# Feed-forward in sevens: one modulation step per pair, two thirds of the steps in the down projection, and the queries' reload in eight parts

## The chip, the cores and the metric

The program runs on one core of one Trainium2 chip. The metric is the time of one execution on the device, in microseconds; the median of three executions is given, and one more execution was recorded by the hardware profiler. Times inside an execution count from its first instruction.

## The reference

Two transformer blocks stand one behind the other on 1024 tokens of width 1024, all in float32. Cut to what the change touches:

```python
# block 1, its feed-forward (D_FF = 2816 = 22 tiles of 128)
xn = rms_norm(x, ffn_norm_g)
gate, up = jnp.split(xn @ w_gate_up, 2, axis=-1)
x = x + (jax.nn.silu(gate) * up) @ w_down
# block 2
mod = silu(c) @ w_mod + b_mod            # 6 vectors of 1024; 2 of them also for c_ctx
h = modulate(rmsnorm(x, norm1_g), sh1, sc1)
q, k, v, u, gb, gc, ga, gcv = split_projection(h @ w_in)
o = latent_window_attention(rope(q), rope(k), v, k_ctx, v_ctx, sink)
y = gb * conv3(gc * u)                   # short convolution
x = x + g1 * ((sigmoid(ga) * (o @ w_proj_attn) + sigmoid(gcv) * (y @ w_proj_conv)) @ w_out)
x = x + g2 * expert_choice_moe(modulate(rmsnorm(x, norm2_g), sh2, sc2), ...)
return rmsnorm(x, final_norm_g)
```

## The kernel before, in words

Everything is written out by hand: the order of the program is the order in which each engine's queue, the DMA queues of SP and GpSimd among them, is worked off. An engine goes on as soon as what its next instruction waits for is there. A matrix product in float32 is three products of parts: every operand is split into a high part (ScalarE, L58) and a rest (VectorE, L59), and `mm3` (L64 to L67) issues high x high, high x rest and rest x high. `Weights` holds the weights' pipeline: SP loads them into stage tiles (L132), `conv` splits them into `wh` and `wl`, `ahead` units before TensorE needs them.

The stages around the change, in order:

- **Gate-up** (L1186 to L1240). The 22 hidden tiles `hr` are made one after the other, f = 0 to 21. The first three (f < `NCL`) are plain products. From f = 3 on a tile and its gate are made as a pair by `quads` (L314): a 2 x 2 block product in seven products of quarters (12 matmuls each, 84 for a pair) instead of eight. Sums of the weights' quarters are GpSimd's (`seven`, L158 to L164), the sums of the seven results VectorE's (L319 to L324 and `plus`, L335), the factor `rsb` GpSimd's again (L1227), the Silu ScalarE's (L1231). The last two products that make the hidden tile (`hidden_out`, L1149 and L1150) are written a pair later (`flush`); then GpSimd stores it to `d_h`. For the last tile they come after the loop.
- **Modulation.** `w_mod` has twelve column blocks s of 512. A step is one load of two row tiles (`mod_load`, L1098, SP's queue, two buffers `mw`) and its use: per row tile one VectorE operation on an accumulator `acc` (L1109 or L1111). For s < 4 there are two accumulators, so a step is four operations, else two. Four steps make a column block; then `mod_sum` lets TensorE add over the partitions (L1120, eight passes for each accumulator) and VectorE add the bias (L1121). `mod_next` uses the step loaded last and loads the next. In the pairs `mods1` does it after product 1, and for f < 11 after product 3 as well, until 24 of the 48 steps are loaded.
- **Down projection** (L1271 to L1302). The hidden tiles come in five parts of 5, 5, 4, 4 and 4. Each part is loaded from `d_h` (`h_load`, three buffers), split (`h_in`) and multiplied with its rows of `w_down`, four columns of 128 at a time (`c0` = 0 and 4, called a chunk below), in pieces of two tiles (`p0` = 0, 2, 4) by `columns_k` (L288). All eight banks are added into `x1` at the end of a chunk (L1288). Between the columns c = 1 and 3 of a piece `mod_next` or, in the second chunk, `step` (split of the next part's tiles) is called; after each chunk follow the sums that are due. The last part is a stage of its own (L1362), for which the modulation must be there.
- **End of the convolution** (L1548 to L1577). In the last four pairs of products (`j` = 0 to 3, gates of the merge) the eight tiles y of the convolution are loaded back from `d_y` (`y_load`, L1553, SP's queue; two buffers, named `z` and `y`) and split (`y_split`).
- **Projection of the convolution** (L1647 to L1674). `gc_load` loads gates on SP's queue. GpSimd's queue loads the keys `kn`, the queries `qn` (4 MB in one transfer, L1651), masks, and later the values `v`. The first two columns are made by `columns_k`, the others by `columns`; `prep_k` and `prep_q` prepare the attention that follows at 1905 us.

Of the kernel before, what the change touches and what calls it, by code (L numbers as in the profile page):

```python
# [8 lines left out]
F32 = mybir.dt.float32  # L9
F32R = mybir.dt.float32r  # L10
# [8 lines left out]
P = 128  # L19
# [3 lines left out]
def fused(tc, x, mix_norm_g, w_in, b_f, sgu_ln_g, sgu_ln_b, w_s, b_s, out_norm_g, w_out,  # L23
# [4 lines left out]
    nc = tc.nc  # L28
# [4 lines left out]
    NT = T // P  # L33
# [1057 lines left out]
        rstd_of(rs1, ss1, D)  # L1091

    modq, modr = deque(), deque()
    acc_of = {}

    def mod_load(s, k):
# [4 lines left out]
    def mod_use(s, k, t):  # L1101
        for j in ((0, 1) if s < 4 else (0,)):
            if k == 0:
                acc_of[s, j] = pmo.tile([P, 512], F32, name=f"acc{j}", bufs=2 - j)
            a = acc_of[s, j]
            for kk in range(2):
                sc = s2[:, k + kk, j:j + 1]
                if k + kk == 0:
                    DVE.tensor_scalar(a, t[:, kk, :], sc, None, op0=OP.mult)  # L1109
                else:  # L1110
                    DVE.scalar_tensor_tensor(a, t[:, kk, :], sc, a, op0=OP.mult, op1=OP.add)  # L1111
        if k == 6:
            modr.append(s)
# [41 lines left out]
    def stores():  # L1155
        while stored:
            stored.popleft()()

    def mod_next(left=0):

        if mwq:
            mod_use(*mwq.popleft())
        if len(modq) > left:
            mod_load(*modq.popleft())

    def early(f):
        if f < FF - 1:
            W.presum()
        else:
            for _ in range(2):  # L1170
                h_load(next(nxt))
# [8 lines left out]
    def mods1():  # L1180

        if modr:
            mod_sum(modr.popleft())
        mod_next(24)

    for f in range(FF):  # L1186
        hr_ = phr.tile([P, T], F32, name="hr")

        def ev_gate(hf, ps):
            g = hr_[:, hf * 512:(hf + 1) * 512]  # L1190
            DVE.tensor_tensor(g, rsb[:, hf * 512:(hf + 1) * 512], ps, op=OP.mult)
            act(g, g, AF.Silu)

        def ev_up(hf, ps):
            g = hr_[:, hf * 512:(hf + 1) * 512]
            DVE.tensor_tensor(g, g, ps, op=OP.mult)
            DVE.tensor_tensor(g, g, rsb[:, hf * 512:(hf + 1) * 512], op=OP.mult)

        if f == 0:
            columns_k(W, 2, xh, xhl, range(KD), lambda c, hf, ps: (ev_gate, ev_up)[c](hf, ps),  # L1200
                      mid={(FM[0], 1): ffn_rs, (FM[1], 1): lambda: spread(rsb, rs1), (FM[2], 1): lambda: W.prime(1)})
            es_fw.close()
            es_x1.close()
            es_T = ExitStack()
            pT = pool(es_T, "pTx", 1, R)
            TX.update({i: quarter(pT, f"t{i}") for i in (4, 1, 2, 3)})
        elif f < NCL:
            columns(W, xh, xhl, KD, ev_gate)
            quarters_x(2 * f - 2)
            if f == NCL - 1:  # L1210
                W.ahead = 4
            columns(W, xh, xhl, KD, ev_up)
            quarters_x(2 * f - 1)
            if f == NCL - 1:
                es_12.close()
                pmo = pool(es_mo, "pmo", 2)
                op = lambda t: [(lambda k, a=a: a[:, k, :]) for a in t]
                SEVX = [op(XQ[0, 0]), op(XQ[1, 0]), op(TX[2]), op(TX[1]), op(TX[3]), op(XQ[1, 1]), op(TX[4])]
        else:
            if f == FF - 1:  # L1220
                W.ahead = 2
            while flush:
                flush.popleft()()
            c1, c2 = halft("c1"), halft("c2")

            def times(x, cs):
                POOL.tensor_tensor(x, x, rsb[:, cs], op=OP.mult)  # L1227
                return x

            def gate(x, cs):  # L1230
                act(x, times(x, cs), AF.Silu)  # L1231

            su = {}
            quads(W, SEVX, halft, lambda s, b: gate(plus(c1, s, b), h0),
                  lambda u, b: (gate(plus(u, u, b), h1), su.update(u=u)),
                  lambda s, b: (times(plus(s, s, b), h0), su.update(s=s)), lambda s, b: times(plus(c2, s, b), h1),
                  {1: mods1, 2: lambda: (stores(), early(f)), **({3: mods1} if f < NCL + 8 else {})})
            flush.append(lambda hr_=hr_, c1=c1, c2=c2, su=su, f=f: hidden_out(hr_, c1, c2, su, f))
        if f < NCL:
            nc.gpsimd.dma_start(d_h[f], hr_)  # L1240
    while flush:
        flush.popleft()()
    W.spare.clear()
    stores()
    assert len(modq) == 24 and not modr and not mwq
    es_mo.close()
    es_xq.close()
    es_T.close()
    es_s1.close()

# [2 lines left out]
    x1 = [px1.tile([P, T], F32, name=f"x1_{k}") for k in range(KD)]  # L1253
    rs1b = px1.tile([P, T], F32, name="rs1b")
    phh = pool(es_f, "phh", 5, R)
    pmo = pool(es_mo, "pmo2", 2)

    def h_split():
        h, l = phh.tile([P, T], F32R, name="hH"), phh.tile([P, T], F32R, name="hL")
# [4 lines left out]
    def h_in():  # L1264
        r = h_split()
        for f in nxt:
            h_load(f)
            break
        return r

    hTs = []  # L1271
    for i, (f0, n) in enumerate(parts):
        hT = [h_in() for _ in range(n)] if not i else hTs
        hv = lambda i: (lambda k, hf: hT[k][i][:, hf * 512:(hf + 1) * 512])
        if f0 + n == FF:
            break
        for c0 in (0, 4):
            if not i:
                for k in range(c0, c0 + 4):
                    nc.gpsimd.dma_start(x1[k], d_xs[k])  # L1280
            hn, nn = [], parts[i + 1][1]

            def step(p0):

                while len(hn) < min(nn, p0 + 5 - n):
                    hn.append(h_in())

            columns_k(W, 4, hv(0), hv(1), range(n), lambda c, hf, ps: DVE.tensor_tensor(  # L1288
                x1[c0 + c][:, hf * 512:(hf + 1) * 512], x1[c0 + c][:, hf * 512:(hf + 1) * 512], ps, op=OP.add), 2,
                mid={(p0, c): (lambda p0=p0: step(p0)) if c0 and c == 3 else mod_next for p0 in range(0, n, 2) for c in (1, 3) if i or c0})  # L1290
            if c0:
                step(n)

            while modr:
                mod_sum(modr.popleft())
        hTs = hn
    while modq or mwq:
        mod_next()
# [251 lines left out]
    def y_load():  # L1550
        k = len(ys) + len(yraw)
        t = pcv.tile([P, T], F32, name="y") if k % 2 else pcv.tile([P, T + 2], F32, name="z")[:, :T]
        nc.sync.dma_start(t, d_y[k])  # L1553
        yraw.append(t)

    def y_split():
# [90 lines left out]
    bank = lambda: psb.tile([P, 512], F32, name="b")  # L1647
    gc_load(0)
    gc_load(1)
    nc.gpsimd.dma_start(kn, d_kv[:, :, :256])  # L1650
    nc.gpsimd.dma_start(qn, d_q)  # L1651
    nc.gpsimd.dma_start(mk, amask_h)
    nc.gpsimd.dma_start(mk0[:, :256], amask_h[:, :256])
    nc.gpsimd.dma_start(mk0[:, 256:], amask_h[:, 384:])
# [9 lines left out]
    columns_k(W, 2, yr, yrl, range(KD), ev_mc)  # L1664
    for j in range(2, 8):
        gc_load(j)
        columns(W, yr, yrl, KD, lambda hf, ps: ev_mc(j, hf, ps))
        for t in ((2 * j - 4, 2 * j - 3) if j < 7 else ()):
            v_in(t)
        if j in (3, 4, 5):  # L1670

            prep_k(0, 4 * j - 12, bank)
        if j == 6:
            prep_q(0, 0, 0, bank)  # L1674
# [625 lines left out]
```

## Time and profile before

| | us |
|---|---|
| median of three executions | 3029.29 (3028.01 to 3029.31) |
| profiled execution | 3026.69 |
| its span, first to last instruction | 3024.9 |
| TensorE busy | 2842.8 (94%) |
| VectorE busy | 2093.8 (69%) |
| ScalarE busy | 1414.8 (47%) |
| GpSimd busy | 851.4 (28%) |
| mean granted TensorE clock | 0.971 of full speed |

In the profile PE is TensorE, DVE is VectorE, ACT is ScalarE, POOL is GpSimd, SP is SyncE; a q behind a name is the engine's queue. Matmuls are pipelined: one starts 0.227 us after the other and is shown 0.39 us long, so that starts are to be compared with starts.

### The profile page before, as it was taken

The numbers are of one execution on the slowest core, as the hardware profiler recorded it, in microseconds if no ns is written. First come the engines' busy times: TensorE is split into PE (matmuls) and PEld (weight loads), VectorE is DVE, ScalarE is ACT, GpSimd is POOL, SyncE is SP. The second block draws the span as 40 slices with busy tenths as digits, with TensorE's granted clock in tenths as the row PEclk, the third lists the DMA queues.
The fourth block names the chain that finished last, engine by engine and source line by source line (L and its number), as shares of the span: only waits on it lengthen the run. The fifth ranks groups of instructions, "written<-read, shape, count | busy, mean of one in ns | idle before, by whom it ended". The sixth has DMA issues, their size and how long they took to land.

```text
span 3024.9 us, 37545 instructions
## 1 busy us (share of the span) xinstructions
PE 2842.8 (94%) x13715; PEld 2366.9 (78%) x13715; DVE 2093.8 (69%) x2925; ACT 1414.8 (47%) x2241; POOL 851.4 (28%) x797
## 2 busy tenths in 40 slices
PE   8999999978999899999999998899999889999996
PEld 7887878767777778778888887777778768888885
DVE  4446844877776456776766652789742479999998
ACT  5346933222222211431333331688721468888886
POOL 1301312355566100325444421133221301211113
PEclk9999999989999999999999999999999899999998
DMA  5120143223332544232222256000254589999997
GB/s 199 36 77 22 41 148 98 81 95 104 105 102 89 202 164 140 91 137 86 91 84 84 84 175 216 21 20 17 83 177 145 194 315 371 377 372 377 377 377 281
DMA packets 303880, 472.76 MB, mean 156 GB/s; under 512 B 15260, under 2 KB 144000, under 8 KB 303568
## 3 DMA queue, kind: packets, MB, share of 16 engines
q1 hardware_dynamic: 281216, 391.27, 37.5%
q0 software_dynamic: 20992, 78.04, 7.4%
q8 instruction: 108, 1.77, 0.2%
q10 hardware_dynamic: 1488, 1.06, 0.1%
q14 instruction: 76, 0.62, 0.1%
HBM read 396.35 MB, written 73.96 MB: 155 GB/s over the span
## 4 chain that ended last, share of the span: by engine, by line
PE 46%; DVE 5%; ACT 2%; DMA 2%; issue 2%; POOL 1%; POOLq 0%; SPq 0%; DVEq 0%; ACTq 0%
PE b L67 13%; PE b L66 13%; PE b L65 13%; PE pt L1760 1%; PE b L2141 1%; PE po L1790 1%; DVE pl L1778 1%; DVE wl L59 1%; DVE sm L1741 1%; PE po L1791 1%; DVE qs L1645 1%; DMA z<-d_y 1%; PE b L1983 0%; DMA ot<-d_o 0%; PE sp L1730 0%
## 5 line engine op out<-in xcount | busy, mean ns | idle before, releaser
L59 DVE TENSOR_TENSOR wl<-wst,wh 128x1024 fp32r<-128x1024 f32 (+2 forms) x677 | 768.9, 1163 | 209.3 <-ACT wh L58 201.4
L58 ACT ACTIVATE wh<-wst 128x1024 fp32r<-128x1024 f32 (+2 forms) x677 | 610.8, 921 | 406.8 <-PE b L66 210.5
L65 PE MATMUL b<-wh,a 128*128 128x512 f32 x768 | 302.0, 393 | 0.2 <-ACT a L58 0.2
L66 PE MATMUL b<-wl,a 128*128 128x512 f32 x768 | 299.4, 390 | 0.8 <-DVE wl L59 0.8
L67 PE MATMUL b<-wh,a 128*128 128x512 f32 x768 | 299.3, 390 | 0.4 <-DVE a L59 0.4
L2183 POOL DMA_INDIRECT d_x<-b,idxT x15 | 65.8, 4387 | 470.7 <-DVE b L2177 470.7
L67 PEld LDWEIGHTS b<-wh,a 128*128 128x128 f32 x768 | 144.2, 188 | 31.0 <-DVE a L59 1.1
L66 PEld LDWEIGHTS b<-wl,a 128*128 128x128 f32 x768 | 144.4, 188 | 30.4 <-DVE wl L59 1.6
L65 PEld LDWEIGHTS b<-wh,a 128*128 128x128 f32 x768 | 144.5, 188 | 29.6 <-ACT a L58 0.7
L65 PE MATMUL b<-xn,wh 128*128 128x512 f32 x368 | 145.0, 394 | 7.3 <-ACT xn L58 6.4
L67 PE MATMUL b<-xn,wl 128*128 128x512 f32 x368 | 144.4, 393 | 2.0 <-DVE wl L59 2.0
L66 PE MATMUL b<-xn,wh 128*128 128x512 f32 x368 | 144.4, 392 | 0.5 <-DVE xn L59 0.5
L65 PE MATMUL b<-hH,wh 128*128 128x512 f32 x352 | 140.5, 399 | 4.4 <-DVE x L1288 2.3
L66 PE MATMUL b<-hL,wh 128*128 128x512 f32 x352 | 139.2, 395 | 4.0 <-DVE hL L59 4.0
L67 PE MATMUL b<-hH,wl 128*128 128x512 f32 x352 | 139.0, 395 | 0.0
L1111 DVE SCALAR_TENSOR_TENSOR acc<-mw,s,acc 128x512 f32<-128x512 f32 x112 | 114.5, 1031 | 23.8 <-DMA mw<-in_w_mod_dram 21.6
L59 DVE TENSOR_TENSOR wl<-ws,wh 128x512 fp32r<-128x512 f32 x78 | 53.5, 688 | 79.8 <-ACT wh L58 79.8
L1741 DVE CUSTOM_DVE_ANT_0 sm<-sp,mk,nsk 128x640 f32<-128x640 f32 (+1 forms) x128 | 107.1, 838 | 1.5 <-PE sp L1730 1.3
L1778 DVE TENSOR_TENSOR pl<-pt,ph 128x512 fp32r<-128x512 f32 x152 | 102.0, 686 | 8.3 <-ACT ph L1770 7.7
L1227 POOL TENSOR_TENSOR c<-c,s 128x512 f32<-128x512 f32 x38 | 63.2, 1662 | 148.6 <-DVE c L335 139.1
L1748 ACT ACTIVATE sm<-sm,tn 128x640 f32<-128x640 f32 (+1 forms) x128 | 103.0, 805 | 0.5 <-DVE tn L1741 0.3
L1760 PE MATMUL pt<-ident,sm 128*128 128x128 f32 x608 | 90.8, 277 | 8.0 <-DVE qs L1645 7.6
(669 smaller groups left out, 7577.3 us busy)
## 6 DMA issues: line engine op xcount, KB each, us to landing
wst<-in_w_exp_gate_dram SPq DMA_DIRECT2D x128, 512.0 KB
wst<-in_w_exp_up_dram SPq DMA_DIRECT2D x128, 512.0 KB
wst<-in_w_exp_down_dram SPq DMA_DIRECT2D x128, 512.0 KB
wst<-in_w_in_dram SPq DMA_DIRECT2D x74, 512.0 KB
mw<-in_w_mod_dram SPq DMA_DIRECT2D x48, 512.0 KB
wst<-in_w_gate_up_dram SPq DMA_DIRECT2D x44, 512.0 KB
d_h<-hr POOLq DMA_DIRECT2D x22, 512.0 KB, 3.0
hr<-d_h SPq DMA_DIRECT2D x22, 512.0 KB
```

The source lines that it names most:

```text
L58: act(h, src, AF.Copy)
L59: DVE.tensor_tensor(l, src, rd(h), op=OP.subtract)
L65: PE.matmul(ps, lh, rh, start=start, stop=False)
L66: PE.matmul(ps, lh, rl, start=False, stop=False)
L67: PE.matmul(ps, ll, rh, start=False, stop=stop)
L1111: DVE.scalar_tensor_tensor(a, t[:, kk, :], sc, a, op0=OP.mult, op1=OP.add)
L1227: POOL.tensor_tensor(x, x, rsb[:, cs], op=OP.mult)
L1741: DVE.tensor_tensor_reduce(sms[n][:, :nk], sps.pop(n)[:, 256:256 + nk], (mk if i else mk0)[:, :nk], -0.125, nsk[:, hd:hd + 1], op0=OP.add, ...
L1748: act(sms[n][:, :nk], sms[n][:, :nk], AF.Exp, bias=m, scale=-1.0, accum_out=s)
L1760: PE.transpose(pt[:, hh * P:(hh + 1) * P], sms[4 * u + hh][:, kb * P:(kb + 1) * P], ident)
L1778: DVE.tensor_tensor(pl, pt, rd(ph), op=OP.subtract)
L2183: nc.gpsimd.indirect_dma_start(out=d_x2, out_offset=bass.IndirectOffsetOnAxis(ap=idxT[:, e:e + 1], axis=0), in_=y, in_offset=None, compute ...
```

## The change

In the pairs of the gate-up stage `mods1` is called once (after product 1) instead of twice in the first eight, and 16 steps are loaded there instead of 24; a column block's sum is thereby written a pair after its last step. The other 32 steps go to the down projection: three calls of `mod_next` after the columns 0, 1 and 2 of a piece (in the second chunk column 3 keeps `step`), none in a chunk's last piece and none in the first chunk of all. The accumulators there have eight buffers, and all eight sums stand behind the last chunk. At the turn between the two stages the first two hidden tiles are split ahead of the last tile's products and in halves. The y tiles are loaded through GpSimd's queue, `kn` through SP's; `qn` goes through SP's queue in eight parts, two behind the gate load of each of the columns 2 to 5.

```diff
+    ACCS = 2
...
-                acc_of[s, j] = pmo.tile([P, 512], F32, name=f"acc{j}", bufs=2 - j)
+                acc_of[s, j] = pmo.tile([P, 512], F32, name=f"acc{j}", bufs=ACCS - j)
...
-        mod_next(24)
+        mod_next(32)
...
-                  {1: mods1, 2: lambda: (stores(), early(f)), **({3: mods1} if f < NCL + 8 else {})})
+                  {1: mods1, 2: lambda: (stores(), early(f))})
...
-    while flush:
-        flush.popleft()()
     W.spare.clear()
-    stores()
-    assert len(modq) == 24 and not modr and not mwq
+    assert len(modq) == 32 and not modr and not mwq
     es_mo.close()
-    es_xq.close()
     es_T.close()
...
-    pmo = pool(es_mo, "pmo2", 2)
+
+    hT0 = [[phh.tile([P, T], F32R, name=x) for x in ("hH", "hL")] for _ in range(2)]
+    for cs in (h0, h1):
+        for k in range(2):
+            split(hT0[k][0][:, cs], hT0[k][1][:, cs], hraw[k][:, cs])
+    while flush:
+        flush.popleft()()
+    stores()
+    es_xq.close()
+    for k in range(2):
+        hraw.popleft()
+        h_load(next(nxt))
+    pmo, ACCS = pool(es_mo, "pmo2", 2), 8
...
-        hT = [h_in() for _ in range(n)] if not i else hTs
+        hT = hTs if i else hT0 + [h_in() for _ in range(n - 2)]
...
-                mid={(p0, c): (lambda p0=p0: step(p0)) if c0 and c == 3 else mod_next for p0 in range(0, n, 2) for c in (1, 3) if i or c0})
+                mid={(p0, c): (lambda p0=p0: step(p0)) if c == 3 else mod_next for p0 in range(0, n, 2) for c in range(4)
+                     if (c0 if c == 3 else (i or c0) and p0 + 2 < n)})
             if c0:
                 step(n)
-
-            while modr:
-                mod_sum(modr.popleft())
...
-        nc.sync.dma_start(t, d_y[k])
+        nc.gpsimd.dma_start(t, d_y[k])
...
-    nc.gpsimd.dma_start(kn, d_kv[:, :, :256])
-    nc.gpsimd.dma_start(qn, d_q)
+    nc.sync.dma_start(kn, d_kv[:, :, :256])
...
         gc_load(j)
+        for t in range(2 * j - 4, min(2 * j - 2, NT)):
+            nc.sync.dma_start(qn[:, t, :], d_q[:, t, :])
         columns(W, yr, yrl, KD, lambda hf, ps: ev_mc(j, hf, ps))
```

## Rows read from the trace of the kernel before

**Rows 1.** The page, busy time of the engines over the span.
```profile
PE 2842.8 (94%) x13715; PEld 2366.9 (78%) x13715; DVE 2093.8 (69%) x2925; ACT 1414.8 (47%) x2241; POOL 851.4 (28%) x797
```

**Rows 2.** TensorE's timeline: start, us, what, wait before it; x00h begins a pair.
```profile
582.80 0.39 PE L65 MATMUL b<-x00h,wh 128*128 128x512 f32 x1
...
621.75 1.84 PE L1120 MATMUL b<-ones,acc 128*128 128x1 f32 x8 [6.51 <-DVE acc L1111]
...
740.68 0.39 PE L65 MATMUL b<-x00h,wh 128*128 128x512 f32 x1
...
759.72 0.39 PE L65 MATMUL b<-x00h,wh 128*128 128x512 f32 x1
...
968.60 0.39 PE L65 MATMUL b<-x00h,wh 128*128 128x512 f32 x1
```

**Rows 3.** VectorE's timeline in the gate-up stage, same columns.
```profile
592.81 0.68 DVE L335 TENSOR_TENSOR c<-s,b 128x512 f32<-128x512 f32 x1
...
602.81 2.98 DVE L1111 SCALAR_TENSOR_TENSOR acc<-mw,s,acc 128x512 f32<-128x512 f32 x4
...
773.95 0.68 DVE L335 TENSOR_TENSOR c<-s,b 128x512 f32<-128x512 f32 x1
774.55 5.98 DVE L1111 SCALAR_TENSOR_TENSOR acc<-mw,s,acc 128x512 f32<-128x512 f32 x4
...
790.13 0.69 DVE L59 TENSOR_TENSOR wl<-ws,wh 128x512 fp32r<-128x512 f32 x1 [3.02 <-ACT wh L58]
...
796.80 0.68 DVE L335 TENSOR_TENSOR c<-s,b 128x512 f32<-128x512 f32 x1
...
797.53 1.59 DVE L1109 TENSOR_SCALAR acc<-mw,s 128x512 f32<-128x512 f32 x1
...
961.69 0.68 DVE L335 TENSOR_TENSOR c<-s,b 128x512 f32<-128x512 f32 x1
...
979.60 0.69 DVE L335 TENSOR_TENSOR c<-s,b 128x512 f32<-128x512 f32 x1 [0.72 <-ACT s L319]
```

**Rows 4.** Timelines of VectorE and TensorE at the turn to the down projection.
```profile
996.27 0.68 DVE L1149 TENSOR_TENSOR hr<-u,c 128x512 f32<-128x512 f32 x1
...
998.72 2.35 DVE L59 TENSOR_TENSOR hL<-hr,hH 128x1024 fp32r<-128x1024 f32 x2
...
999.99 0.80 PE L66 MATMUL b<-hL,wh 128*128 128x512 f32 x1 [3.99 <-DVE hL L59]
```

**Rows 5.** Timelines of TensorE and VectorE: a sum among the pairs, then the down projection.
```profile
953.96 0.94 PE L1120 MATMUL b<-ones,acc 128*128 128x1 f32 x8
...
1087.04 1.54 DVE L1111 SCALAR_TENSOR_TENSOR acc<-mw,s,acc 128x512 f32<-128x512 f32 x2 [3.96 <-DMA mw<-in_w_mod_dram]
...
1089.23 3.57 PE L1120 MATMUL b<-ones,acc 128*128 128x1 f32 x16 [4.29 <-DVE x L1288]
...
1216.40 1.86 PE L1120 MATMUL b<-ones,acc 128*128 128x1 f32 x8 [3.36 <-DVE acc L1111]
1218.13 0.77 PE L65 MATMUL b<-hH,wh 128*128 128x512 f32 x1
```

**Rows 6.** Convolution's end: timelines; two windows; landing of the d_xs loads (L1280).
```profile
1785.39 1.30 POOL L164 TENSOR_TENSOR wst<-wst,ws 128x512 f32<-128x512 f32 x1
...
1808.38 0.55 POOL L1651 DMA_DIRECT2D qn<-d_q  x1
...
1808.87 0.34 SPq L1553 DMA_DIRECT2D z<-d_y  x1
...
1825.54 1.06 ACT L58 ACTIVATE xn<-z 128x1024 fp32r<-128x1024 f32 x1 [17.02 <-DMA z<-d_y]
...
1805.00:1819.80 14.80, 14.38 (x63) 11.93 (x64) 3.32 (x4) 2.53 (x3) 3.61 (x6) 1.00 1.02 373
1819.80:1840.00 20.20, 11.85 (x37) 8.53 (x37) 8.47 (x9) 5.18 (x5) 1.08 (x2) 0.75 0.65 260
...
DMA to landing us min/median/max: 6.4/12.5/19.1
```

## The prediction, made before the changed kernel was run

> **What bounds the kernel now.** I read the page first: TensorE is busy for most of the span [rows 1], so a gain can only come from the places where it waits. Then I read TensorE's timeline between 560 and 1910 us, each start against the one before, which shows four such places. For each I read the timeline of the engine that TensorE waited for.
>
> *The pairs of the gate-up stage.* A pair of hidden tiles is 84 matmuls; undisturbed it takes 759.72 - 740.68 = 19.04 us, or 0.2267 us a matmul [rows 2]. The 17 pairs f = 4 to 20 take 968.60 - 582.80 = 385.8 us, 22.7 each. The eye falls on the modulation sums: at 621.75 TensorE has waited 6.5 us for `acc`, and there are four such places. But the bound is another one. VectorE's line L335 (`c<-s,b`, the first of a pair) stands in every pair, and its starts are VectorE's period [rows 3]: 796.80 - 773.95 = 22.85 us in the pair with one step of four operations (f = 11), 979.60 - 961.69 = 17.9 us in a pair without a step, and more than both where there are two steps. In the pair of 22.85 VectorE waits for ScalarE (3.02 us at 790.13, behind GpSimd's products and a Silu) and never for TensorE. VectorE's queue, with these waits in it, sets the pace; a TensorE stall at a sum is mostly time it would have waited for `wl` anyway.
>
> *The turn to the down projection.* VectorE first writes the last hidden tile (996.27) and only then splits the first one (998.72); the first product with `hL` starts at 999.99 [rows 4].
>
> *The down projection.* From 999.99 to 1218.13 are 218.1 us for 864 matmuls, which need 195.9 [rows 4, 5]. Of the 22.2 us lost, some 2 lie at the start (estimate: ten matmuls at half clock, as the 0.80 of the first shows) and 1218.13 - (1216.40 - 3.36) = 5.1 at the last sum. The other 15.1 lie where one chunk ends and the next begins: the most at 1089.23, where two sums waited 4.29 us and ran 3.4 at the low clock (VectorE had sat 3.96 us waiting for `mw` at 1087.04, so the banks were read late), and smaller ones at the others.
>
> *The end of the convolution.* `qn` (4 MB) is issued at 1808.38, the load of y tile 6 (named `z`) at 1808.87; ScalarE gets that tile at 1825.54, after 17 us [rows 6]. In 1805 to 1819.8 the DMA engines are full at 373 GB/s.
>
> **The change part by part.**
>
> *Gate-up: one step per pair.* Removed are eight steps of two VectorE operations (s = 4, 5), and the second step of eight pairs. A second step lay after quarter product 3, where GpSimd is idle: four operations in 2.98 us. A step after product 1 takes 5.98, since GpSimd's sums run beside it [rows 3]. All 16 steps that stay are of the dear kind with four operations, and the pairs f = 12 to 19, which had two operations each, now have four. So I count on VectorE's clock. In the pair f = 3 the step (577 to 579.9, 2.8 us) goes: the mark of f = 4 moves from 592.81 to 590.1. Then 12 pairs at 22.85. Four pairs begin a column block with a scalar product, which took 1.59 us beside GpSimd at 797.53; three of these also carry a sum: 23.2 (estimate). Then one pair of 17.9. The mark of f = 21 comes at 590.1 + 274.2 + 92.8 + 17.9 = 975.0, before at 979.60: 4.6 us gained, far less than the waits at the sums seem to promise. The sums themselves come when `acc` has been done for a pair's length: no wait, 1.9 us of TensorE, covered by its slack of 3.8 us a pair. If a pair is 0.4 us off, that is 6.4 us: ends -2 and 11. In the last pair TensorE reaches product 4 just when its weights are ready instead of waiting for them at the low clock; bounds 0 to 2 us, I take 1.
>
> The Trainium skill (SBUF — State Buffer, section "SBUF: two separate sides") says that a VectorE operation with two SBUF inputs and a GpSimd operation that reads SBUF lock each other out for a whole instruction. This speaks against the change, which moves every step into GpSimd's stretch; the 5.98 against 2.98 above agrees in kind, and how far it could go is the third rival.
>
> *Splits ahead of the last hidden tile, in halves.* The first split then starts where the write stood, at 996.27, and the half that is needed first ends 0.7 us later: TensorE goes on at 996.97, 3.0 us earlier. The store of the last tile comes some 1.2 us later, and behind it on GpSimd's queue the loads of `x1`; they are needed by the sums into `x1` after 1025, so that is covered. The loads of hidden tiles 2 and 3 wait for the splits of 0 and 1, which end about 2 us earlier. Bounds 1 and 4.
>
> *Down projection: three steps in a full piece, none in a chunk's last piece, sums at the end.* A piece is 48 matmuls, 10.9 us. A step of two operations takes 1.54 us and a load some 4.3 us after its buffer is free (3.96 was waited at 1087.04) [rows 5]. With two buffers three steps end about 9.7 us after a piece begins, six in two pieces at 20.6 of 21.8. The last piece has only VectorE's weight split, tile splits and bank reads, so the banks are read in time. Of the 15.1 I leave 0.6 for what stays: 14.5 gone. Behind the `mw` loads on SP's queue stand weight and hidden tile loads; they have a piece or more of slack, and what is left of it late would show in the 0.6. Against this stands the end. Three steps and eight sums are left: the last load waits for the step that reads its buffer, 3.3 us after the last matmul, and takes 4.3; its step ends at about 9.2, the last sum at 10.3. Seven sums (0.94 us each at full clock, 953.96) run in that time. Before, the gap there was 5.1. So 5.2 are lost again: the part gains 9.3, I take 9. Ends: eight sums at the low clock (1.73 each, 1216.40 to 1218.13) make the gap 14 and the gain 5.5; a gap as before makes it 14.5.
>
> *Queries' reload and the y loads.* With `qn` gone from 1808, y 6 and 7 have the DMA engines nearly to themselves. They now go through GpSimd's queue; eight loads of this size on that queue landed after 6.4 (the first) to 19.1 us [rows 6]. Taking 6.4 as the upper bound, y 6 lands by 1815.3 and is split by 1817.7; its products come at 1820. The stretch 1819.8 to 1840 holds 37 matmuls, 8.4 us of work at full speed, at a clock of 0.75 [rows 6]; 11.8 us are lost, of which 1.7 (estimate for a weight split behind the bank reads) stays: 10.1 gained. Two costs: on GpSimd the y loads wait for splits and stand ahead of the product at 1785.39 (L164), so that one weight conversion comes later; I take 1.0 us of it at the start of the next stage (estimate: one split of a y tile, 1.06 us as at 1825.54; bounds 0 and two of them). And `kn` and the eight parts of `qn` stand on SP's queue ahead of weight loads: each column of 10.9 us then moves about 2.75 MB, 252 GB/s, under the 373 seen. No cost taken, 2 us if that cover is thin. Gain 9.1, ends 5 and 10.5.
>
> **Sum.** 4.6 + 1 + 3.0 + 9 + 9.1 = 26.7 us. The profiled execution took 3026.69 us, 1.8 more than its span, and would take 3000.0; the median of the runs shown is 2.6 us higher, so for the median I say 3029.29 - 26.7 = 3002.6.
>
> **The rivals.**
>
> *TensorE's sum stalls were the bound.* Then every pair falls to the 19.04 us of an undisturbed one, and the pairs gain up to 385.8 - 17 x 19.04 = 62.1 instead of 5.6 (which includes f = 3 and the last pair): 3002.6 - 56.5 = 2946 at the best. For it: TensorE's wait is booked to `acc`. Against it: VectorE's period shows no wait for TensorE. Chance 0.06.
>
> *A gain is taken back.* The sums at the end run slowly and the banks come late in each chunk all the same (down projection gains 0 instead of 9: 3011.6), or the y tiles on GpSimd's queue come as late as now (3011.7). Against: the waits named above vanish in program order. Chance 0.18 for one of them.
>
> *Slower: the steps cost VectorE a whole GpSimd instruction each.* If each of the four operations waits for one GpSimd product (1.3 us, as the one at 1785.39) before its 0.75, the step takes 8.2 instead of 5.98 and a pair 25.1: 16 x 2.2 = 35.6 more, 3038. It decides from 24.5 us a pair on (26.7 / 16 above 22.85), and is slower by 0.2% from 24.9. The skill's rule named above, taken at its word, gives this; the pair at 773.95 shows less. Chance 0.05.
>
> **How the numbers follow.** The forecast has 0.71: 3002.6, alone within 2993 to 3011 by the bounds above (not all at one end at once). The second rival lies at 3012, so the range is 2992 to 3014. A measurement of this kernel tells about 0.2%, 6 us, from no change; faster than 3023 are the forecast and the first two rivals, less a part of the tails: 0.92; same 0.04, slower 0.04.
>
> **What would show it.** Right: L335's marks 22.5 to 23.5 us apart from f = 4 to 19, with no wait for TensorE between them, and TensorE waiting for `wl` there instead of `acc`; the first `hL` product 1 to 2 us after the first `hH` product; no wait over 0.5 us between the chunks, then a gap of 9 to 12 us with the sums in it; the y tile split before 1820 less what was gained, and the matmuls there at full clock. Wrong: marks under 21 or over 24.5; a gap at the sums over 14; ScalarE waiting for `z` still; TensorE waiting at the attention's start for `qn`.

## The result, and the profile after

The changed kernel takes 3011.68 us (median of five executions, 3008.91 to 3013.13), the kernel before 3028.53 in the same measurement: a ratio of 0.9945, 95% interval 0.993 to 0.9959. 16.9 us are gained where 26.7 were forecast. The profiled execution took 3008.91 us (span 3007.1), 17.8 less than the one of before.

Where the 17.8 us come from, by the same marks in both traces:

| from, to | before | after | gained | forecast |
|---|---|---|---|---|
| start to the first product with `hL` | 999.99 | 992.13 | 7.9 | 8.6 |
| to the last part of the down projection | 218.1 | 216.2 | 1.9 | 9 |
| to the attention's first scores | 686.4 | 677.0 | 9.4 | 9.1 |
| to the end of the span | 1120.4 | 1121.8 | -1.4 | 0 |

So one part is off, the down projection. The last row is no effect of the change: the expert products (from the transposes of the first expert's rows to the last product behind them), which no edit here touches, took 566.2 us before, 567.8 after, and 566.3 to 569.0 in the runs below.

The page's busy times, to be held against [rows 1]: TensorE 7.6 us less busy in a span 17.8 us shorter, VectorE 13.6 us more; the mean granted clock is 0.976 instead of 0.971.

```profile
PE 2835.2 (94%) x13715; PEld 2360.4 (78%) x13715; DVE 2107.4 (70%) x2927; ACT 1414.3 (47%) x2243; POOL 852.5 (28%) x803
```

**The pairs.** VectorE's timeline in the changed kernel, one pair from the mark L335 to the next (columns as in [rows 2]; L1112 is the modulation step, L1111 of before), and TensorE's wait in the pair before:

```profile
819.31 0.68 DVE L335 TENSOR_TENSOR c<-s,b 128x512 f32<-128x512 f32 x1
819.91 6.00 DVE L1112 SCALAR_TENSOR_TENSOR acc<-mw,s,acc 128x512 f32<-128x512 f32 x4
825.83 1.75 DVE L59 TENSOR_TENSOR wl<-wst,wh 128x512 fp32r<-128x512 f32 x1
...
835.51 0.69 DVE L59 TENSOR_TENSOR wl<-ws,wh 128x512 fp32r<-128x512 f32 x1 [3.01 <-ACT wh L58]
...
842.20 0.68 DVE L335 TENSOR_TENSOR c<-s,b 128x512 f32<-128x512 f32 x1
...
804.74 0.50 PE L67 MATMUL b<-t4h,wl 128*128 128x512 f32 x1 [3.50 <-DVE wl L59]
```

The pair takes 842.20 - 819.31 = 22.89 us, like the one of [rows 3] with four operations, and every pair from f = 4 to 19 takes 22.8 to 22.95 (the first 22.4). TensorE never waits for `acc` there any more, as it did in [rows 2]; it waits for `wl` instead.

**The down projection.** Timelines in the changed kernel: TensorE's long waits; then VectorE, ScalarE and SP's queue ahead of the first of them:

```profile
992.13 0.50 PE L66 MATMUL b<-hL,wh 128*128 128x512 f32 x1 [1.44 <-DVE hL L59]
...
1051.80 0.76 PE L65 MATMUL b<-hH,wh 128*128 128x512 f32 x1 [2.74 <-DVE x L1297]
...
1110.54 0.47 PE L65 MATMUL b<-hH,wh 128*128 128x512 f32 x1 [2.62 <-DVE x L1297]
...
1197.70 8.29 PE L1121 MATMUL b<-ones,acc 128*128 128x1 f32 x56
...
1206.62 1.87 PE L1121 MATMUL b<-ones,acc 128*128 128x1 f32 x8 [0.62 <-DVE acc L1112]
1208.34 0.77 PE L65 MATMUL b<-hH,wh 128*128 128x512 f32 x1
...
1033.65 1.23 DVE L59 TENSOR_TENSOR wl<-wst,wh 128x1024 fp32r<-128x1024 f32 x1 [1.57 <-ACT wh L58]
1034.79 1.53 DVE L1112 SCALAR_TENSOR_TENSOR acc<-mw,s,acc 128x512 f32<-128x512 f32 x2
1040.79 1.54 DVE L1112 SCALAR_TENSOR_TENSOR acc<-mw,s,acc 128x512 f32<-128x512 f32 x2 [4.47 <-DMA mw<-in_w_mod_dram]
...
1043.43 2.35 DVE L59 TENSOR_TENSOR hL<-hr,hH 128x1024 fp32r<-128x1024 f32 x2
...
1048.51 2.55 DVE L59 TENSOR_TENSOR hL<-hr,hH 128x1024 fp32r<-128x1024 f32 x2 [1.58 <-ACT hH L58]
1050.97 4.87 DVE L1297 TENSOR_TENSOR x<-x,b 128x512 f32<-128x512 f32 x8
...
1047.41 1.06 ACT L58 ACTIVATE hH<-hr 128x1024 fp32r<-128x1024 f32 x1 [2.92 <-DMA hr<-d_h]
...
1034.90 0.37 SPq L132 DMA_DIRECT2D wst<-in_w_down_dram  x1
1035.32 7.40 SPq L1099 DMA_DIRECT2D mw<-in_w_mod_dram  x3
1042.78 2.24 SPq L1179 DMA_DIRECT2D hr<-d_h  x2
```

The sums no longer stand between the chunks ([rows 5]: 4.29 us waited at 1089.23). But at the ends of the two second chunks with five tiles TensorE waits 2.74 and 2.62 us for the banks. Some 4.4 and 2.8 us are lost there: behind the first wait the products also run slowly (granted clock 0.51 from 1051.8 to 1055, the level of 1.2 GHz), behind the second it is 1.00. Read backwards from the first: the banks are read late (1050.97) because the split of two hidden tiles (1048.51) is late; that waits for ScalarE, which waits for a hidden tile's load; this was issued after 1042.78, behind three `mw` loads; and on VectorE the splits that free its buffer stand behind a step that waited 4.47 us for `mw`. The first of the three `mw` loads was issued at 1035.32, right behind a weight load on SP that had to wait for its own buffer (read until 1034.9), though a buffer for `mw` had been free for about three us. At the second end the same rows stand: VectorE waits 1.79 us (at 1106.95) for ScalarE, which had waited 2.50 for a hidden tile.

**The convolution's end.** ScalarE's timeline: the tile that came after 17 us in [rows 6] is there before TensorE needs it.

```profile
1805.19 1.06 ACT L58 ACTIVATE xn<-z 128x1024 fp32r<-128x1024 f32 x1 [6.53 <-DMA z<-d_y]
```

### The profile page after: what moved, and what is told of

It reads as the page before. It is cut to its first block, busy times and chain, and to the rows that moved or that the text cites. A ratio compares the mean times of both kernels' runs of the same rounds, so it can differ in the third digit from the quotient of the medians.

```text
span 3007.1 us, 37555 instructions
## 1 busy us (share of the span) xinstructions
PE 2835.2 (94%) x13715; PEld 2360.4 (78%) x13715; DVE 2107.4 (70%) x2927; ACT 1414.3 (47%) x2243; POOL 852.5 (28%) x803
## 4 chain that ended last, share of the span: by engine, by line
PE 44%; DVE 6%; issue 2%; ACT 2%; DMA 2%; POOL 1%; SPq 0%; POOLq 0%; DVEq 0%; ACTq 0%
PE b L67 13%; PE b L66 13%; PE b L65 13%; PE pt L1768 1%; PE b L2149 1%; DVE pl L1786 1%; DVE wl L59 1%; DVE sm L1749 1%; PE po L1798 1%; DVE qs L1652 1%; PE po L1799 1%; DMA ot<-d_o 0%; PE b L1991 0%; DMA v<-d_kv 0%; DMA g<-d_gc 0%
## 5 line engine op out<-in xcount | busy, mean ns | idle before, releaser
L59 DVE TENSOR_TENSOR wl<-wst,wh 128x1024 fp32r<-128x1024 f32 (+2 forms) x677 | 759.7, 1149 | 163.3 <-ACT wh L58 155.6
L1112 DVE SCALAR_TENSOR_TENSOR acc<-mw,s,acc 128x512 f32<-128x512 f32 x112 | 127.7, 1148 | 33.6 <-DMA mw<-in_w_mod_dram 30.8
## 6 DMA issues: line engine op xcount, KB each, us to landing
wst<-in_w_exp_gate_dram SPq DMA_DIRECT2D x128, 512.0 KB, 10.8
wst<-in_w_exp_up_dram SPq DMA_DIRECT2D x128, 512.0 KB, 10.8
wst<-in_w_exp_down_dram SPq DMA_DIRECT2D x128, 512.0 KB, 10.8
```

Source lines behind the costliest of these rows:

```text
L59: DVE.tensor_tensor(l, src, rd(h), op=OP.subtract)
```

## The experiments

All ratios are against runs of the kernel before on the same chip. Their intervals are mostly some 10 us wide, so where a few us matter the stage is read from the trace.

**Are the sums the bound? The kernel before without them in the pairs.**

```diff
-    def mod_sum(s):
+    def mod_sum(s, skip=False):
...
+            if skip:
+                DVE.tensor_copy(modT[:, j, 4 * s:4 * s + 4], vecT[:, V_BMOD + 4 * s:V_BMOD + 4 * s + 4])
+                continue
...
-            mod_sum(modr.popleft())
+            mod_sum(modr.popleft(), True)
```

> The kernel before with the TensorE sums of the modulation left out in the pairs (VectorE copies the bias alone into the modulation's columns there, so these four blocks of the modulation lack their matrix product; the steps on VectorE all stay). Theory (a pair is as long as a chain of hand-overs with the steps' time on VectorE in it, and the 6.5 us that TensorE waited at a sum it would have waited for weights): the eight pairs with two steps stay at 25.4 to 26.8 us, so 0 to 8 us less, 0.9973 to 1.000 of before. Rival (TensorE's stall at the sums makes the pairs long): the four pairs with such a sum lose 6 to 8 us each, and the time falls by 25 to 57 us, 0.981 to 0.992.

Measured: 1.0013 (1.0004 to 1.0023), just above the theory's range. By VectorE's marks the pairs with two steps take 25.4 to 25.8 us still, and the seven from f = 4 to 10 together 179.2 instead of 181.1. What makes the time longer lies in a place that this edit doesn't touch: from the context's first product to the attention's first scores it takes 646.3 us instead of 638.9, most of it lost where the queries are reloaded. TensorE's timeline, at the place of [rows 2] where the sum had waited 6.51 us:

```profile
624.48 0.51 PE L67 MATMUL b<-t4h,wl 128*128 128x512 f32 x1 [3.75 <-DVE wl L59]
```

The wait has only changed its name. The rival is gone: nearly all of what the trace books to `acc` was time that TensorE would have waited for weights.

**The step behind the fourth product, where GpSimd is idle.**

```diff
-                  {1: mods1, 2: lambda: (stores(), early(f))})
+                  {3: mods1, 2: lambda: (stores(), early(f))})
```

> The changed kernel with its one modulation step per pair put behind the fourth product instead of the second; nothing else moves. Theory (VectorE's own program sets a pair, and a step's four two-input operations are slow only where GpSimd multiplies beside them: 5.98 us behind the second product, 2.98 behind the fourth in the trace of before): the step falls from 5.98 to about 3.0 us and the pair from 22.87 to 19.9 to 20.9 us, TensorE's 84 products alone being 19.04, so 16 pairs give 31 to 47 us: 0.979 to 0.985 of the kernel before, against 0.9945 with the step behind the second product. Rival 1 (TensorE's wait for the sum's input sets the pair): there is one sum in four pairs either way, no change, 0.994 to 0.995. Rival 2 (the slow reads follow the step wherever it lies): no change either, but the step's operations stay at about 1.5 us each in the trace.

Measured: 0.9929 (0.9912 to 0.9945), and the pairs take 22.4 to 22.9 us: the theory, which the prediction shared ("the dear kind"), falls. VectorE's timeline in one pair, and ScalarE's:

```profile
729.43 1.19 DVE L59 TENSOR_TENSOR wl<-wst,wh 128x512 fp32r<-128x512 f32 x1 [2.59 <-ACT wh L58]
...
732.85 3.42 DVE L1112 SCALAR_TENSOR_TENSOR acc<-mw,s,acc 128x512 f32<-128x512 f32 x4
...
742.41 0.69 DVE L59 TENSOR_TENSOR wl<-ws,wh 128x512 fp32r<-128x512 f32 x1 [3.02 <-ACT wh L58]
...
741.23 0.63 ACT L1232 ACTIVATE u<-u 128x512 f32<-128x512 f32 x1 [8.78 <-POOL u L1228]
741.76 0.61 ACT L58 ACTIVATE wh<-ws 128x512 fp32r<-128x512 f32 x1
```

The step did become short, 3.42 us instead of 6.00. But where it had stood VectorE now waits 2.59 us for ScalarE. VectorE is busy 15.5 of 23 us here and 18.1 with the step behind the second product, and the pair takes the same time: neither its work nor TensorE's 19.04 us is the bound, but a ring of hand-overs. VectorE's `c` goes to GpSimd's product, that to ScalarE's Silu, behind which on ScalarE's queue stands the next weight split, which VectorE needs for `wl`. A step behind the second product lies in that wait for 2.6 of its 6 us; behind the fourth it lies in none. That this ring is the bound was only argued here; the next two runs test it.

**The step cut in two, a half in each of VectorE's two long waits.**

```diff
...
-        mod_next(32)
+        if mwq:
+            half.append(mwq.popleft())
+            mod_use(*half[0], (0,))
+        if len(modq) > 32:
+            mod_load(*modq.popleft())
...
+    def mods2():
+        if half:
+            mod_use(*half.pop(), (1,))
...
-                  {1: mods1, 2: lambda: (stores(), early(f))})
+                  {1: mods1, 2: lambda: (stores(), early(f)), 5: mods2})
```

> The changed kernel with each modulation step of the pairs cut in two: its first two operations stay behind the second product, the other two go behind the sixth. Same operations. With the step behind the fourth product the trace had VectorE waiting 2.59 us for ScalarE behind the second product and 3.02 behind the sixth, and a pair took 22.9 all the same. New theory (a pair is a chain of hand-overs among VectorE, GpSimd and ScalarE; the part of a step that lies in a wait costs nothing, the rest lengthens the chain by itself: 5.98 less 2.6 behind the second product, 3.42 behind the fourth): two operations of some 1.5 us fit each of the two waits, so a pair falls from 22.87 to the 19.0 to 20.3 that pairs without a step take; 16 pairs give 40 to 60 us, 0.974 to 0.982 of before. Rival (VectorE's work itself, some 16 to 18 us busy with its fixed waits, sets the pair wherever it lies): no change, 0.993 to 0.995.

Measured: 2980.25 us, 0.9841 (0.9824 to 0.9857); 31 us under the changed kernel. A pair takes 20.97 us (21.46 in every fourth, with a sum), more than the 19.0 to 20.3 expected. Timelines of VectorE and GpSimd in a pair:

```profile
801.88 0.68 DVE L335 TENSOR_TENSOR c<-s,b 128x512 f32<-128x512 f32 x1
802.47 2.44 DVE L1112 SCALAR_TENSOR_TENSOR acc<-mw,s,acc 128x512 f32<-128x512 f32 x2
805.58 1.20 DVE L59 TENSOR_TENSOR wl<-wst,wh 128x512 fp32r<-128x512 f32 x1 [0.67 <-ACT wh L58]
...
812.62 2.88 DVE L1112 SCALAR_TENSOR_TENSOR acc<-mw,s,acc 128x512 f32<-128x512 f32 x2
816.16 0.69 DVE L59 TENSOR_TENSOR wl<-ws,wh 128x512 fp32r<-128x512 f32 x1 [0.67 <-ACT wh L58]
...
822.85 0.68 DVE L335 TENSOR_TENSOR c<-s,b 128x512 f32<-128x512 f32 x1
...
802.64 1.73 POOL L1238 TENSOR_TENSOR c<-c,s 128x512 f32<-128x512 f32 x1 [3.15 <-DVE c L335]
...
813.21 1.74 POOL L1238 TENSOR_TENSOR u<-u,s 128x512 f32<-128x512 f32 x1
```

Behind both halves VectorE still waits 0.67 us for ScalarE: the halves fit. What a pair is without any step was measured next.

**The changed kernel without steps in the pairs.**

```diff
-        if modr:
-            mod_sum(modr.popleft())
-        mod_next(32)
+        if mwq:
+            s, k, t = mwq.popleft()
+            if k == 6:
+                for j in (0, 1):
+                    DVE.tensor_copy(modT[:, j, 4 * s:4 * s + 4], vecT[:, V_BMOD + 4 * s:V_BMOD + 4 * s + 4])
+        if len(modq) > 32:
+            mod_load(*modq.popleft())
```

> The changed kernel without the modulation steps of the pairs and their sums (four blocks of the modulation lack their matrix product and get the bias alone); the weights are still loaded, nothing else changes. It measures what a pair takes without a step: 22.87 us with the step in one piece, 20.98 with the half steps. Theory (the half steps lie in waits that VectorE has anyway, 0.67 us of each is left in front of the next weight split): a pair without any step takes 20.2 to 21.0 us. Rival (the half steps still lengthen the chain, only less): 19.0 to 19.8 us, as TensorE's 84 products alone take 19.04.

Measured: 0.9804 (0.9779 to 0.9828); a pair takes 20.09 us, between the two ranges. The same timelines:

```profile
830.95 0.68 DVE L335 TENSOR_TENSOR c<-s,b 128x512 f32<-128x512 f32 x1
834.22 1.20 DVE L59 TENSOR_TENSOR wl<-wst,wh 128x512 fp32r<-128x512 f32 x1 [2.59 <-ACT wh L58]
...
844.35 0.69 DVE L59 TENSOR_TENSOR wl<-ws,wh 128x512 fp32r<-128x512 f32 x1 [3.02 <-ACT wh L58]
...
851.05 0.68 DVE L335 TENSOR_TENSOR c<-s,b 128x512 f32<-128x512 f32 x1
...
831.71 1.29 POOL L1232 TENSOR_TENSOR c<-c,s 128x512 f32<-128x512 f32 x1 [3.16 <-DVE c L335]
...
841.85 1.28 POOL L1232 TENSOR_TENSOR u<-u,s 128x512 f32<-128x512 f32 x1
```

So the ring alone takes 20.09 us, more than TensorE's 19.04. A whole step adds 2.8 to it in either place: 3.8 us behind the second product and 3.3 behind the fourth, less 0.5 for each weight split (two and one) that then comes when GpSimd's sums are over and takes 0.68 instead of 1.18 us. The halves add 0.88, and the rows put this on GpSimd: beside a half its product for `c` takes 1.73 instead of 1.29 us, and the one for `u` 1.74 instead of 1.28. The rest of the pair is equally long in both traces, within 0.01 us. No run separates it.

**The queries alone.** In the kernel before, only the reload of `kn` and `qn` is moved to SP, `qn` in eight parts; the y loads stay on SP.

```diff
-    nc.gpsimd.dma_start(kn, d_kv[:, :, :256])
-    nc.gpsimd.dma_start(qn, d_q)
+    nc.sync.dma_start(kn, d_kv[:, :, :256])
...
+        for t in range(2 * j - 4, min(2 * j - 2, NT)):
+            nc.sync.dma_start(qn[:, t, :], d_q[:, t, :])
```

> The kernel before with one part of the change alone: the queries' and keys' reload from SP, the queries in eight parts between the columns; the y loads stay on SP's queue. Theory (the 4 MB of queries filled the DMA engines at 373 GB/s when the last y tiles were to come): ScalarE no longer waits 17 us for the tile, TensorE's stretch at low clock there goes, and as the y loads are not moved to GpSimd no weight conversion is late: 9 to 10.5 us less, 0.9965 to 0.9970 of before. Rival (the y tile is late because of its place on SP's queue): the wait for the tile stays over 10 us and the gain is under 4, 0.9987 to 1.000.

Measured: 0.9966 (0.9954 to 0.9979), 10.3 to 10.8 us. ScalarE's wait for the tile fell to 7.61 us, and TensorE's wait for it is gone; from the context's first product to the first scores this run takes 630.2 us, the changed kernel 629.8, the one before 638.9. ScalarE's timeline:

```profile
1815.66 1.06 ACT L58 ACTIVATE xn<-z 128x1024 fp32r<-128x1024 f32 x1 [7.61 <-DMA z<-d_y]
```

The reload was the whole cause: the 4 MB of the queries, with the keys' 1 MB that moved along and that no run separates. That the y loads moved to GpSimd's queue shows neither a gain nor a cost beyond 0.4 us.

**The down projection: four single edits.** In order: the splits ahead of the steps; the hidden tiles' loads on GpSimd's queue; a third `mw` buffer; and the `mw` loads on GpSimd's queue.

```diff
-                mid={(p0, c): (lambda p0=p0: step(p0)) if c == 3 else mod_next for p0 in range(0, n, 2) for c in range(4)
-                     if (c0 if c == 3 else (i or c0) and p0 + 2 < n)})
+                mid={(p0, c): (lambda p0=p0: step(p0)) if c == 0 else mod_next for p0 in range(0, n, 2) for c in range(4)
+                     if (c0 if c == 0 else (i or c0) and p0 + 2 < n)})
```

> The changed kernel with the order inside a pair of hidden tiles of the down projection turned round: the splits of the next part's hidden tiles behind the first column, and the three modulation steps behind the second to fourth. Same instructions, other order. Theory (the waits of 2.74 and 2.62 us before the last reads of the banks at the ends of the two chunks come from hidden tiles that are split late, because the splits that free their buffers stand on VectorE behind modulation steps that wait for weights, and their loads on SP behind those weights' loads): the two waits vanish, and the slow clock behind them, 5 to 7 us less than the changed kernel: 0.9920 to 0.9930 of the kernel before. Rival (VectorE simply has too much to do there): the same operations take the same time, no change, 0.994 to 0.995, and the waits stand.

```diff
...
-            h_load(f)
+            h_load(f, nc.gpsimd)
```

> The changed kernel with the reloads of the hidden tiles in the down projection issued by GpSimd, which has nothing else to do there, instead of SP; the order on VectorE stays. Theory A (SP's queue is the cause: the reloads stand behind modulation weights that wait for their two buffers): the waits of 2.74 and 2.62 us at the chunk ends vanish, 5 to 7 us less than the changed kernel, 0.9920 to 0.9930 of before. Theory B (VectorE's order is the cause: the split that frees a hidden tile's buffer stands behind steps that wait for modulation weights): the reloads wait for the same buffers on the other queue, 0 to 2 us less, 0.9938 to 0.9945. Rival (VectorE has too much to do): no change.

```diff
-    pmo, ACCS = pool(es_mo, "pmo2", 2), 8
+    pmo, ACCS = pool(es_mo, "pmo2", 3), 8
```

> The changed kernel with three buffers instead of two for the modulation weights in the down projection. Theory (both forms of the one above): the loads wait less for a buffer, so that VectorE's steps no longer wait 4.47 and 2.86 us for weights, and the splits behind them come 3 to 4 us earlier: the waits at the chunk ends shrink from 2.74 and 2.62 to under 1, 3 to 7 us less than the changed kernel, 0.9920 to 0.9935 of before; of the gap at the end of the down projection (10.4 us) perhaps 1 to 3 us go too, as its last loads start earlier. Rival (VectorE has too much to do there): no change at the chunk ends.

```diff
...
-        nc.sync.dma_start(t, wsrc(w_mod_2[0], k, 2, s * 512, 512))
+        MODQ.dma_start(t, wsrc(w_mod_2[0], k, 2, s * 512, 512))
...
-    pmo, ACCS = pool(es_mo, "pmo2", 2), 8
+    pmo, ACCS, MODQ = pool(es_mo, "pmo2", 2), 8, nc.gpsimd
```

> The changed kernel with one edit: the down projection's modulation weights are loaded from GpSimd's queue; two buffers and the order of steps and splits as in the changed kernel. With splits first and three buffers besides, the stage took 207.5 us instead of 216.2. Theory 1 (the place of the loads on SP's queue is the one cause, the other two edits did nothing before it and add little to it): the waits before the bank reads at the chunk ends fall under 0.8 us and the stage takes 207 to 210.5 us, 6 to 9 us less than the changed kernel, 0.9915 to 0.9925 of before. Theory 2 (three late chains side by side, each of them enough to keep the banks waiting): the waits of 2 us stay, the stage takes 213 to 217 us, 0.9935 to 0.9945.

| edit | ratio | stage, us | waits at the two chunk ends, us |
|---|---|---|---|
| none (the changed kernel) | 0.9945 | 216.2 | 2.74, 2.62 |
| splits first | 0.9939 (0.9922 to 0.9955) | 215.1 | 2.06, 2.81 |
| hidden tiles on GpSimd's queue | 0.9952 (0.9933 to 0.9971) | 217.5 | 2.40, 1.93 |
| three `mw` buffers | 0.9937 (0.9921 to 0.9954) | 215.0 | 2.09, 2.93 |
| `mw` on GpSimd's queue | 0.9938 (0.9921 to 0.9954) | 221.6 | 2.73, 5.79 |

No single edit removes the waits; the last even lengthens one, and its stage of 221.6 us lies outside the ranges of both its theories. Each time the trace names another late operation. VectorE's timeline with the splits first: it is the step again, at 1041.52, 5.65 us late by `mw`:

```profile
1041.52 1.54 DVE L1112 SCALAR_TENSOR_TENSOR acc<-mw,s,acc 128x512 f32<-128x512 f32 x2 [5.65 <-DMA mw<-in_w_mod_dram]
```

**Splits first and three buffers together.**

> The changed kernel with both edits of the down projection together: hidden tiles split behind the first column, and three buffers for the modulation weights. Alone, each left waits of 2.1 to 2.9 us before the bank reads at the chunk ends: with the splits first, VectorE stood 5.65 us for modulation weights before the splits of the last piece; with three buffers, the hidden tiles' loads still waited for their splits behind the steps. Theory (two chains are late by about the same, and each hides the other): together the waits at both chunk ends fall under 0.8 us, 5 to 7 us less than the changed kernel in the stage, 0.991 to 0.993 of before. Rival (VectorE has too much to do in a chunk of five tiles, in whatever order): waits of 2 us and more stay, 0.9935 to 0.9945.

Measured: 0.9937 (0.9921 to 0.9954), stage 215.4 us, waits of 1.94, 1.43 and 3.16: this theory falls too. Timelines of SP's queue and VectorE:

```profile
1029.43 0.37 SPq L132 DMA_DIRECT2D wst<-in_w_down_dram  x1
1029.84 1.76 SPq L1179 DMA_DIRECT2D hr<-d_h  x2
1031.70 1.81 SPq L1099 DMA_DIRECT2D mw<-in_w_mod_dram  x3
...
1038.66 1.54 DVE L1112 SCALAR_TENSOR_TENSOR acc<-mw,s,acc 128x512 f32<-128x512 f32 x2 [5.54 <-DMA mw<-in_w_mod_dram]
```

Now the buffers are free early, but SP reaches the three loads at 1031.70 only, since the weight load ahead of them waits for its stage tile until 1029.4 and the second of two hidden tiles for its buffer until 1030.6. (The DMA engines stood still for some four us before that, 1026 to 1030, not for the nine that the next expectation says.)

**All three: splits first, three buffers, and `mw` on GpSimd's queue.**

> The changed kernel with the splits first and three buffers, as in the run before, and the down projection's modulation weights loaded from GpSimd's queue, which has nothing else to do there. In the run before, VectorE still stood 5.5 us for modulation weights in front of the last piece's splits: SP issued them at 1031.70, only when the weight and hidden tile loads ahead of them had got their buffers at 1029.4, and three of them with two hidden tiles took 7 us to land, after nine us in which the DMA engines had moved nothing. Theory (the modulation weights stand behind those loads on SP, though their own buffers are free): on a queue of their own they land before their steps, VectorE's waits for them fall under 1 us, the waits before the bank reads at the two chunk ends (2.74 and 2.62 us in the changed kernel) under 0.8, and the gap at the end of the down projection falls from 10.4 to 8 to 9.5 us, as its last three loads are under way earlier: 6 to 9 us less than the changed kernel, 0.9915 to 0.9925 of before. Rival (VectorE has too much to do in a chunk of five tiles): the steps come earlier but the waits of 2 us stay, 0.9932 to 0.9945.

Measured: 0.9898 (0.9883 to 0.9913); the stage takes 207.5 us, 8.7 less than in the changed kernel, and no wait for a bank is left at a chunk's end. VectorE reads the banks at once, and TensorE's gap at the end is 1197.01 - 1188.25 = 8.8 us, the eight sums alone, instead of 1208.34 - 1197.70 = 10.6. Timelines of VectorE and TensorE:

```profile
1042.42 1.23 DVE L59 TENSOR_TENSOR wl<-wst,wh 128x1024 fp32r<-128x1024 f32 x1 [3.17 <-ACT wh L58]
1043.56 2.35 DVE L59 TENSOR_TENSOR hL<-hr,hH 128x1024 fp32r<-128x1024 f32 x2
1045.83 4.87 DVE L1298 TENSOR_TENSOR x<-x,b 128x512 f32<-128x512 f32 x8
...
1188.25 8.90 PE L1122 MATMUL b<-ones,acc 128*128 128x1 f32 x64
1197.01 0.77 PE L65 MATMUL b<-hH,wh 128*128 128x512 f32 x1
```

The steps have their weights when it is their turn. The view of the waits shows it over the whole stage; these are the rows of VectorE waiting for `mw` in the changed kernel (total us, times, longest):

```profile
DVE acc L1112 <- DMA mw<-in_w_mod_dram: 30.8, 9, 4.6
DVE acc L1110 <- DMA mw<-in_w_mod_dram: 14.8, 4, 5.2
```

The same view of the run with `mw` on GpSimd's queue and two buffers:

```profile
DVE acc L1113 <- DMA mw<-in_w_mod_dram: 27.1, 9, 4.7
DVE acc L1111 <- DMA mw<-in_w_mod_dram: 13.5, 3, 6.4
```

That is 45.6 and 40.6 us; with three buffers and the splits first on SP's queue it is 51.3, and with all three edits that view has no such row. So the free queue alone doesn't help, nor the third buffer and the order without the queue. Whether the order is needed besides the other two was not tried, nor the queue with the order and two buffers. Of the 15 us between this run and the changed kernel the stage has 8.7; the rest lies in stages that the edits don't touch (2.7 us before this one, 5.2 behind the attention's first scores) and is no effect of them.

**Half steps and all three.**

> The half steps in the pairs together with all three edits of the down projection of the run above. They lie in different stages, so the gains should add: 31 us (half steps, measured against the changed kernel) and 6 to 9 us: 0.9810 to 0.9825 of before. Rival (the down projection's edits do nothing): 0.983 to 0.985, as the half steps alone.

Measured: 2970.8 us (2967.88 to 2973.21), 0.9812 (0.9798 to 0.9825): the gains add, and this version is 57.6 us under the kernel before, 41 more than the change.

## Why the prediction was right and wrong

- **Gate-up and the turn: right in its sum, wrong in a reason.** 8.6 us forecast, 7.9 measured although the stage began 0.6 us later; the pair of 22.85 came as 22.87, TensorE's waits moved from `acc` to `wl`, and the run without the sums shows that they bound next to nothing (1.9 us in seven pairs). But "All 16 steps that stay are of the dear kind" doesn't hold as a reason: a step costs a pair 2.8 us behind the second product and behind the fourth. The forecast came out because it took the period of a pair from rows instead of adding up steps. Its "17.9 us in a pair without a step" is no such price: only the pair f = 20 takes that, in every run, and where no pair has a step the others take 20.09. "VectorE's queue, with these waits in it" was near; the bound is the ring through GpSimd and ScalarE, in which a step counts only by what of it lies outside a wait.
- **The third rival, 3038 us, is gone:** a step takes 6.00 us and not 8.2. By single operations its four take 0.75, 1.66, 1.93 and 1.66 us, and each of the last three ends 0.55 us behind the end of a GpSimd product (822.35 behind 821.80, 824.21 behind 823.65, 825.91 behind 825.36). So they waited for the rest of a product that was under way, and the first for none, where the rival counted a whole product for all four. The Trainium skill (SBUF — State Buffer, section "SBUF: two separate sides") says that a VectorE operation with two SBUF inputs and a GpSimd operation that reads SBUF lock each other out for a whole instruction. These rows agree. That the step moved to where GpSimd is idle left the pairs at 22.9 us doesn't clear the slowing, as the move took away the wait in which the step lay as well; what an unslowed step behind the second product would cost no run shows.
- **The down projection: the term that was mis-sized.** 9 forecast (5.5 to 14.5 by its bounds), 1.9 measured; the difference is the two chunk ends, some 4.4 and 2.8 us. The gap at the end came as worked out (10.6 against 10.3). What failed is the step "a load some 4.3 us after its buffer is free [...] three steps end about 9.7 us after a piece begins", and with it "Behind the `mw` loads on SP's queue stand weight and hidden tile loads; they have a piece or more of slack". The prediction asked what stands behind the `mw` loads and not what they stand behind: a weight load that waits for its own buffer. In the piece ahead of the first late end the three steps end 10.9 us after it begins (1043.51 - 1032.58), not 9.7; the splits behind them come later by that, and VectorE then stands 1.58 us more for the hidden tile whose load was behind the `mw` loads. A chunk of five tiles has a last piece half as long as the others (5.4 us), in which this can't be made good. The runs show it from the other side: with a queue of their own, a third buffer and the splits ahead the steps are in time, and the stage gives 10.6 us against before, the 9.3 that were worked out and a little more.
- **The second rival is nearest to what came, and its number by luck.** "A gain is taken back", with the down projection's gain at 0, was put at 3011.6 us and 0.18; 3011.68 was measured. The tenth is chance: the part gained 1.9 and not 0, gate-up 0.7 less than forecast, and 1.4 were lost at the end where no edit reaches. The forecast alone was given 2993 to 3011, which just misses it; the range to 3014 holds it because this rival was added. Half of its mechanism was right (the banks come late in a chunk), though at two ends and not at each, and the eight sums at the end took 1.2 us each but for the last with 1.7 (1.1 each with all three edits), so all but the last were far from the 1.73 of the low clock.
- **The queries and the y tiles: right,** 9.4 for 9.1 (9.1 of it from the context's first product on). The cost taken for the moved y loads (1.0 us) doesn't show: the queries alone gave the same within 0.4 us.

## What to carry to other kernels

Where several engines hand work round in a loop, look for the waits that each has in every turn: work put into them is nearly free (0.88 us a turn here), and the same work anywhere else lengthens the loop by most of its length (2.8 of 3.4 us), however short it has become there. For a load, ask what it stands behind on its issuing queue and whether that can wait for a buffer: here a free buffer was worth nothing behind it, and a free queue alone nothing either. If several late chains end at one place, single edits change little and say little; put them together and see whether the engine's wait for the transfer is gone. A smaller total says nothing yet: 40.6 us went with a stage of 221.6, 51.3 with one of 215.4; only at none did it fall.

## What the runs showed of the hardware

- Moving the issue of a load from one queue to another was worth 215.4 - 207.5 = 7.9 us in one stage (with buffers to use it), because the first queue stood still in front of it. The Trainium skill (DMA: Bandwidth & Descriptors, section "Issuing engines are not separate DMA queues") says that issuing on several engines saves only the sequencer's time for starting a DMA, usually little. Here the gain was of another kind, the time that the queue stood waiting for buffers.
- VectorE and GpSimd side by side slow each other: a GpSimd product took 1.73 us instead of 1.29 beside two VectorE operations with two inputs, and these two took 2.44 to 2.88 us, where four took 2.98 alone [rows 3].
